# Second up projection: sixteen units instead of twelve with their weight sums formed in DRAM

## The chip, the cores and the metric

The kernel runs on one core of a Trainium2 chip. Its metric is the device time of one execution in microseconds (us); the time given for a kernel is the median of several runs. One further execution was recorded by the hardware profiler, and all rows of a trace come from that one.

## The reference, cut to what matters

A decoder layer of 512 tokens and model width 1024, in float32. The part that changes is the second feed-forward block; its hidden width is 2816, which is 22 tiles of 128.

```python
D_MODEL, SEQ, D_FF = 1024, 512, 2816

def swiglu(x, w_gate, w_up, w_down):
    return (jax.nn.silu(x @ w_gate) * (x @ w_up)) @ w_down

def reference(x, ...):
    x = x + 0.5 * swiglu(rmsnorm(x, ffn1_norm), ffn1_wg, ffn1_wu, ffn1_wd)
    x = x + hybrid_mixer(rmsnorm(x, mix_norm), w_in, ...)        # attention and a gated recurrence
    x = x + 0.5 * swiglu(rmsnorm(x, ffn2_norm), ffn2_wg, ffn2_wu, ffn2_wd)
    return rmsnorm(x, final_norm)
```

## The kernel before, in words

**Exact products from rounded parts.** TensorE multiplies float32 values that are rounded (float32r). Each operand is split into a rounded part and a remainder: ScalarE copies the rounded part (`wh`), VectorE subtracts to get the remainder (`wl`). A product is then three matmuls: `wh` with the moving rounded part, `wh` with the moving remainder, `wl` with the moving rounded part.

**Stages.** First up projection, first down projection, then the mixer as a list of 64 projections (`ORDER`, numbered 0 to 63, run by `run_jobs`), then the second up projection (`ffn_up` with `blocks`), then the second down projection. An ordinary mixer projection is 24 matmuls of 512 columns.

**The second up projection.** Of its 22 tiles, 4 (`DIRECT2`) are multiplied directly, gate and up, which makes 8 direct projections. The other 18 tiles are taken in pairs by a seven-product block scheme (as Strassen and Winograd do): two pairs of 128 columns of weights form four blocks a11, a12, a21, a22, and the tokens are halved likewise. This gives 18 *units*; each has seven *products*, numbered 1 to 7, and each product needs one block or one sum of blocks: 1 needs a11, 2 a12, 4 a22, 5 s1 = a21 + a22, 6 s2 = s1 + a11, 3 s4 = s2 + a12, and 7 s3 = a21 + a11 (the signs lie in the operands). Products 1, 6, 7 and 4 of a unit use the bank of PSUM called `mm`; 2, 5 and 3 use `aux`. The 18 x 7 = 126 products run in one list, `stream`: product i is issued, then `step(i)` reads the results of product i - 1 and calls `prepare(i + LEAD)` (`LEAD` is 4), which splits the weights of a product four places ahead.

**Two kinds of unit.** Constant `UNITS` says from which unit on the sums are formed in DRAM.

- A unit below it forms its sums in the on-chip memory. `load` has SP issue its loads (a11 and a12, a21 twice, a22: 1.25 MB), POOL adds a22 and a11 onto the two copies of a21 by accumulating DMAs, and VectorE adds s2 and s4 (`add_weights`). Only products 2, 5 and 3 are *wide*. A wide product is, for each of four operand tiles, one matmul of 512 columns (rounded part and remainder lie side by side) and one of 256; a narrow one is three matmuls of 256 columns.
- A unit from it on (`o.blocks`) reads finished sums from DRAM, 256 KB for each product, and all seven products are wide. `fetch_pair` has SP load two products' weights into one 512 KB buffer of a ring of three (`RAWS`); ScalarE and VectorE split the two together, one `wh` and one `wl` of 1024 columns; then the buffer is loaded again, for the pair three further on. Results pass through `copies` and `reads`, in place of `results`: ScalarE first copies the whole bank, VectorE then adds.

**How the DRAM sums are made.** `Blocks.stages` lists 8 DMAs of 256 KB in six dependent stages for a unit, *moves* here; for the second up projection all are issued by POOL. `sums_in_turn` interleaves the units so that two stages of one unit lie two groups apart. `sums_until(part)` issues moves until that part of them is out. It begins with a *beat*: VectorE sets one column of a small tile (8 columns in turn) and POOL copies it, so that POOL can't run ahead of VectorE. It is called at three places: in the mixer from projection `SUMS_FROM` on, twice in each projection, up to `SUMS_PART`, in proportion to the planned time since that projection over `SUMS_TIME`; six times beside the direct projections, up to `SUMS_PART + DIRECT_PART`; and at every second product of the stream, up to all of them at product `SUMS_STEPS`. The first of the six calls stands ahead of the POOL DMAs that complete the moving operands t1, r and q (`Operands.moved`, rows `cm<-ca`, `cm<-cr`, `cm<-cq`), which products 5, 7 and 4 read. The beats and moves are unknown to the planner (`Plan`), which places the mixer's other instructions by estimated times.

The sums of the second down projection's weights are moves too (`scr<-w2d` and `scr<-scr`). They are spread over the projections before `SUMS_FROM` by `run_jobs`; what is left of them is issued at projection `SUMS_FROM - 1`.

Of the kernel before, what the change touches and what calls it, by code (L numbers as in the profile page):

```python
# [44 lines left out]
PLAIN, PAIRS, TAIL = 6, 8, 3  # L45
DIRECT1, DIRECT2 = 4, 4
SUMJOBS = 48
UNITS, SUMS_FROM, SUMS_PART, DIRECT_PART, SUMS_STEPS, SUMS_TIME = 6, 37, 0.8, 0.1, 44, 145


ORDER = """
# [2022 lines left out]
```

## Time and profile before

| | us |
|---|---|
| median of 3 runs (lowest, highest) | 1062.77 (1062.4, 1063.34) |
| the profiled execution, whole | 1061.5 |
| its span, first to last instruction | 1059.7 |
| TensorE busy in the span | 1051.1 (99%) |
| VectorE busy | 884.9 (84%) |
| ScalarE busy | 667.1 (63%) |
| POOL busy | 237.2 (22%) |

Times in rows are counted from the start of the span. The span is 1.8 us shorter than the profiled execution, and that one is 1.3 us under the median. PE is TensorE's matmuls and PEld its weight loads, DVE is VectorE, ACT ScalarE; SPq is SP's queue. Matmuls overlap, so that the pitch from one start to the next tells more than the duration of one.

### The profile page before, as it was taken

What the parts mean: (1) busy time and instruction counts of PE and PEld (TensorE: products, weight loads), DVE (VectorE), ACT (ScalarE), POOL (GpSimd) and SP (SyncE); (2) the same over time, 40 slices, a digit from 0 to 9 for tenths busy, and PEclk for the clock granted to TensorE, in tenths of its full rate; (3) what the DMA queues carried; (4) which work ended last, traced back from release to release, by engine and by line L of the source; (5) the groups of instructions that cost most, each with busy time, mean ns of one, the idle gap of its engine ahead of it and who ended that gap; (6) DMA issues with size and microseconds to landing.
All of it is one profiled execution on the core that took longest, in us unless ns stands there. A gap on an engine that the chain in (4) does not pass through costs nothing.

```text
span 1059.7 us, 16590 instructions
## 1 busy us (share of the span) xinstructions
PE 1051.1 (99%) x5716; PEld 909.6 (86%) x5716; DVE 884.9 (84%) x1742; ACT 667.1 (63%) x1250; POOL 237.2 (22%) x357
## 2 busy tenths in 40 slices
PE   9999999999999999999999999999999999999997
PEld 7889999989999788888888888888899888888885
DVE  6679999989988879999899866865799888878875
ACT  7456656656476657976886664445666666666663
POOL 0261323302131011212031444442732000000020
PEclk9999999999999999999999999999999999999999
DMA  9786999938783477667494878999994666545573
GB/s 326 180 170 159 264 225 231 233 97 236 182 220 122 128 225 171 179 181 188 126 234 123 208 177 198 278 236 261 265 223 100 191 197 197 180 155 167 187 205 122
DMA packets 94548, 205.26 MB, mean 194 GB/s; under 512 B 11776, under 2 KB 18560, under 8 KB 93824
## 3 DMA queue, kind: packets, MB, share of 16 engines
q1 hardware_dynamic: 60720, 136.24, 39.2%
q0 software_dynamic: 33024, 67.13, 32.9%
q8 instruction: 45, 0.74, 0.3%
q10 hardware_dynamic: 720, 0.84, 0.2%
q14 instruction: 39, 0.32, 0.1%
HBM read 194.72 MB, written 48.23 MB: 229 GB/s over the span
## 4 chain that ended last, share of the span: by engine, by line
PE 97%; ACT 1%; DVE 1%; DMA 0%; issue 0%
PE mm L171 68%; PE aux L171 29%; DMA vt<-vec 0%; ACT L171 0%; ACT rl L171 0%; ACT r L171 0%; DVE tu L171 0%; DVE o L171 0%; DVE wl L171 0%; ACT wh L171 0%; DVE tg L171 0%; ACT yh L171 0%; DVE xr L171 0%; DVE sq L171 0%; ACT xc L171 0%
## 5 line engine op out<-in xcount | busy, mean ns | idle before, releaser
L171 DVE TENSOR_TENSOR wl<-wr,wh 128x1024 fp32r<-128x1024 f32 (+2 forms) x233 | 232.2, 1000 | 60.5 <-ACT wh L171 58.8
L171 ACT ACTIVATE wh<-wr 128x1024 fp32r<-128x1024 f32 (+3 forms) x235 | 203.7, 873 | 76.4 <-PE aux L171 24.0
L171 PE MATMUL mm<-cm,wh 128*128 128x256 f32 (+1 forms) x1184 | 240.9, 310 | 0.0
L171 PEld LDWEIGHTS mm<-cm,wh 128*128 128x128 f32 x1184 | 189.3, 191 | 7.3 <-ACT tu L171 0.2
L171 PE MATMUL mm<-cm,wl 128*128 128x256 f32 x736 | 172.5, 282 | 0.0
L171 PE MATMUL mm<-yh,wh 128*128 128x512 f32 (+1 forms) x416 | 163.8, 394 | 0.3 <-ACT i L171 0.2
L171 PE MATMUL mm<-yl,wh 128*128 128x512 f32 (+1 forms) x416 | 162.2, 390 | 0.0
L171 PE MATMUL mm<-yh,wl 128*128 128x512 f32 x408 | 159.2, 390 | 0.0
L171 PEld LDWEIGHTS mm<-cm,wl 128*128 128x128 f32 x736 | 130.0, 190 | 6.1
L171 PE MATMUL aux<-cm,wh 128*128 128x512 f32 (+1 forms) x472 | 122.9, 379 | 0.0
L171 PEld LDWEIGHTS mm<-yh,wh 128*128 128x128 f32 (+1 forms) x416 | 78.0, 187 | 17.1 <-ACT i L171 0.6
L171 PEld LDWEIGHTS mm<-yl,wh 128*128 128x128 f32 (+1 forms) x416 | 77.6, 187 | 15.6 <-DVE yl L171 0.5
L171 PEld LDWEIGHTS mm<-yh,wl 128*128 128x128 f32 x408 | 76.6, 188 | 16.4 <-DVE wl L171 0.2
L171 PEld LDWEIGHTS aux<-cm,wh 128*128 128x128 f32 x472 | 79.7, 189 | 9.4
L171 ACT ACTIVATE wh<-s 128x512 fp32r<-128x512 f32 x96 | 58.8, 625 | 43.3 <-DVE s L171 32.9
L171 DVE TENSOR_TENSOR wl<-s,wh 128x512 fp32r<-128x512 f32 x96 | 65.4, 688 | 14.5 <-ACT wh L171 13.8
L171 PEld LDWEIGHTS aux<-cm,wl 128*128 128x128 f32 x440 | 68.8, 189 | 8.7
L171 PE MATMUL aux<-cm,wl 128*128 128x256 f32 x440 | 74.0, 281 | 0.0
L326 POOL DMA_DIRECT2D scr<-w2d x32 | 29.6, 1003 | 175.5 <-DMA scr<-w2d 163.5
L159 POOL DMA_DIRECT2D s<-w1u x44 | 41.3, 1136 | 114.4 <-DVE wl L171 69.7
L159 POOL DMA_DIRECT2D cm<-h x16 | 13.8, 863 | 207.5 <-ACT cm L171 198.0
L171 PE MATMUL mm<-wh,cm 128*128 128x512 f32 x192 | 59.1, 389 | 0.0
(267 smaller groups left out, 2151.6 us busy)
## 6 DMA issues: line engine op xcount, KB each, us to landing
wr<-scr SPq DMA_DIRECT2D x80, 256.0 KB, 2.9
wr<-wm SPq DMA_DIRECT2D x39, 512.0 KB, 3.9
scr<-w2u POOLq DMA_DIRECT2D x72, 256.0 KB, 6.1
s<-w1u POOLq DMA_DIRECT2D x44, 256.0 KB, 7.6
scr<-scr POOLq DMA_DIRECT2D x40, 256.0 KB, 6.1
wr<-w1u SPq DMA_DIRECT2D x19, 512.0 KB, 6.2
wr<-w1d SPq DMA_DIRECT2D x18, 512.0 KB, 4.2
wr<-w2u SPq DMA_DIRECT2D x36, 256.0 KB, 2.9
```

Source lines behind the costliest of these rows:

```text
L159: return self.engine.dma_start(out, src, **kw)
L171: return call(*args, **kw)
L326: plain, adds = nc.gpsimd.dma_start, lambda o, i: nc.gpsimd.dma_start(o, i, accum_op=ALU.add)
```

## The change

Six constants change, and no other line:

```diff
 SUMJOBS = 48
-UNITS, SUMS_FROM, SUMS_PART, DIRECT_PART, SUMS_STEPS, SUMS_TIME = 6, 37, 0.8, 0.1, 44, 145
+UNITS, SUMS_FROM, SUMS_PART, DIRECT_PART, SUMS_STEPS, SUMS_TIME = 2, 33, 0.68, 0.07, 62, 185
```

Units 2 to 5 become units with sums in DRAM and seven wide products; units 0 and 1 stay as they are. The moves of this projection grow from 12 x 8 = 96 to 16 x 8 = 128. They begin at projection 33 instead of 37, at a lower rate for each us, and end at product 62 of the stream instead of 44. What is left of the down projection's moves is issued at projection 32 instead of 36.

## Rows read from the trace of the kernel before

**Rows 1.** Page, part 1: busy time and share of the span, instructions.

```profile
PE 1051.1 (99%) x5716; PEld 909.6 (86%) x5716; DVE 884.9 (84%) x1742; ACT 667.1 (63%) x1250; POOL 237.2 (22%) x357
```

**Rows 2.** Waits of engine PE over the span: total us, times, longest.

```profile
PE aux L171 <- DVE epst L171: 1.1, 1, 1.1
...
PE mm L171 <- ACT i L171: 0.2, 1, 0.2
```

**Rows 3.** Windows: PE, PEld, DVE, ACT, POOL busy; clock, DMA share, GB/s.

```profile
551.40:573.20 21.80, 21.80 (x102) 18.04 (x101) 21.48 (x42) 17.26 (x31) 0.85 (x3) 1.00 0.49 134
776.60:804.50 27.90, 27.90 (x206) 26.49 (x205) 27.22 (x60) 17.18 (x37) 10.32 (x16) 1.00 0.77 177
850.00:930.00 80.00, 80.00 (x459) 69.91 (x458) 69.65 (x102) 51.59 (x76) 0.00 (x0) 1.00 0.60 189
```

**Rows 4.** Timeline of PE: start, us, operation; a wide product and a narrow one.

```profile
772.33 1.09 PE L171 MATMUL aux<-cm,wh 128*128 128x512 f32 x4
...
773.74 0.40 PE L171 MATMUL mm<-cm,wh 128*128 128x256 f32 x2
...
775.18 0.40 PE L171 MATMUL mm<-cm,wh 128*128 128x256 f32 x2
```

**Rows 5.** Timeline of PE: first matmul of the stream, first after it.

```profile
762.37 0.40 PE L171 MATMUL mm<-cm,wh 128*128 128x256 f32 x2
...
940.02 0.82 PE L171 MATMUL mm<-ident,x 128*128 128x128 f32 x6
```

**Rows 6.** DMA queues and issues, 573 to 717: share of engines; count, size, us to landing.

```profile
q0 software_dynamic: 7275, 19.11, 59.2%
...
scr<-w2u POOLq DMA_DIRECT2D x59, 256.0 KB, 6.0
scr<-scr POOLq DMA_DIRECT2D x16, 256.0 KB, 5.7
...
wr<-w2u SPq DMA_DIRECT2D x5, 512.0 KB, 6.6
```

**Rows 7.** DMA queues and issues, 850 to 930.

```profile
q1 hardware_dynamic: 8281, 15.06, 59.5%
...
wr<-w2u SPq DMA_DIRECT2D x23, 256.0 KB, 2.9
```

**Rows 8.** DMA queues and issues, 663 to 679.

```profile
q0 software_dynamic: 817, 2.13, 56.1%
q1 hardware_dynamic: 751, 2.64, 46.6%
...
wr<-wout SPq DMA_DIRECT2D x6, 512.0 KB, 5.9
```

**Rows 9.** DMA issues, 762.3 to 850.

```profile
cm<-cq POOLq DMA_DIRECT2D x2, 128.0 KB, 9.7
```

**Rows 10.** Timeline of POOL: last move of the down projection's sums, last DMA of q.

```profile
556.12 0.82 POOL L326 DMA_DIRECT2D scr<-w2d  x1 [4.69 <-DMA scr<-scr]
...
763.93 0.86 POOL L159 DMA_DIRECT2D cm<-cq  x1 [1.40 <-ACT cm L171]
```

**Rows 11.** Timeline of all engines: a split that frees a buffer, then load, split, first matmul.

```profile
845.28 1.05 ACT L171 ACTIVATE wh<-wr 128x1024 fp32r<-128x1024 f32 x1
...
847.00 1.22 DVE L171 TENSOR_TENSOR wl<-wr,wh 128x1024 fp32r<-128x1024 f32 x1
...
848.25 3.25 SPq L159 DMA_DIRECT2D wr<-w2u  x3
...
853.49 1.05 ACT L171 ACTIVATE wh<-wr 128x1024 fp32r<-128x1024 f32 x1
...
854.57 1.23 DVE L171 TENSOR_TENSOR wl<-wr,wh 128x1024 fp32r<-128x1024 f32 x1 [0.17 <-PE mm L171]
...
858.62 0.63 PE L171 MATMUL mm<-cm,wh 128*128 128x512 f32 x2
```

**Rows 12.** Tile beat: engine, operation, count, duration min/median/max in ns, first and last start.

```profile
L1074 DVE MEMSET beat<- x62: 59/59/59, 573.1 to 822.4; 128x1 f32 x62
```

## The prediction, made before the changed kernel was timed

> **What bounds the kernel now.** I read the page's busy line first: TensorE's matmuls fill 1051.1 us of the span, 99%, VectorE 84%, ScalarE 63% [rows 1]. A busy PE says little by itself, so I went to the waits of PE: three waits, 1.1, 0.2 and 0.2 us, are all that the trace knows in the whole span, and the longest is at the start [rows 2]. Then the windows around the change: PE is busy in every microsecond of the stretch where the mixer would now start its moves, of the narrow units' stretch and of a stretch of wide units, at full granted clock [rows 3]. So the stream runs as fast as TensorE takes matmuls, and only the number and width of matmuls can shorten it. Last, the pitch of single products in the timeline: a wide one takes 773.74 - 772.33 = 1.41 us, a narrow one 775.18 - 773.74 = 1.44 us [rows 4]. The reader is to see there that three matmuls of 256 columns cost almost what one of 512 and one of 256 cost.
>
> I checked that against the whole stream. It has 126 products and lasts 940.02 - 762.37 = 177.65 us [rows 5]. Units 0 to 5 have four narrow products each, 24 in all. With 24 x 1.44 = 34.6, the other 102 have 143.1 us left, 1.403 each. So the wide pitch over many is 1.403, and there is no idle time left over in the stream to win.
>
> **The change, part by part.**
>
> *Narrow products become wide.* Products 1, 6, 7 and 4 of units 2 to 5: 16 products, 16 x (1.44 - 1.403) = 0.6 us less on TensorE, which is the path. It is the only term that shortens the path.
>
> *VectorE and ScalarE in those units.* On VectorE a unit loses s2 and s4 (two adds of 512 columns) and splits of 512 columns become half as many of 1024; it gains the adds of `reads`. ScalarE gains the copies of whole banks. I don't add it up, since both kinds of unit stand in the trace: the narrow ones keep VectorE busy 27.22 of 27.90 us and ScalarE 17.18, the wide ones 69.65 and 51.59 of 80 [rows 3], so VectorE goes from 98% to 87%, ScalarE from 62% to 64%. Nothing is gained, because PE didn't wait in either; nothing is lost, because the later units already run so.
>
> *More beats.* 62 now [rows 12]. Afterwards up to 62 in the mixer (31 projections, two calls), 6 and 31, so at most 37 more, 37 x 59 ns = 2.2 us of VectorE spread over some 300 us; its 13% of idle time in wide units covers it. In the four projections where beats are new, VectorE is busy 21.48 of 21.80 us [rows 3], and 8 beats need 0.5 us. PE doesn't wait for it there now; without cover it would cost that 0.5 us.
>
> *The mixer's moves.* 75 are issued between 573 and 717 [rows 6], and one more at the edge: 76 of 96. As the part is 0.8 x t / 145, the planned time t at the last call was 141.6 to 143.5 us. Four more projections are 96 matmuls; 102 took 21.8 us there [rows 3], and with the attention's own matmuls between them I put 23 us. So the new count is 128 x 0.68 x 165 / 185 = 77.6, thus 78. Two more moves over 23 us more time: the mixer's loads meet a thinner stream of moves than now, and PE doesn't wait there now. The stretch that becomes new to moves has its DMA engines at 0.49 [rows 3]. The down projection's last moves come at projection 32 in place of 36, but POOL has them out at 556.12 by itself, as their landings allow [rows 10]. The first beats of projection 33, some 23 us before 573.1 [rows 12], wait some 7 us for that; nothing else is queued behind them on POOL, and 8 columns of beats, two to a projection, are 23 us of slack for VectorE. Cost zero; gain zero.
>
> *Beside the direct projections.* The first of six calls brings the moves to 128 x 0.6917, so 89: a burst of 11, where it is now 3 (76 to 79). All six bring it to 96, 18 moves in place of 11. The burst stands on POOL ahead of the DMAs for t1, r and q. From rows 6 a move takes 0.592 x 144 / 75 = 1.14 us of all 16 engines. In return the loads of units 2 to 4 leave this stretch, and those of unit 5 the next. The operand with least room is q: its last DMA is issued at 763.93 and takes some 9.7 us, so it is there at 773.6 [rows 10, 9]; product 4 of unit 0, the twelfth of the stream, starts 6 x 1.44 + 5 x 1.403 = 15.7 us after 762.37, at 778.0. Room 4.4 us. The seven extra moves are 8.0 us of DMA time, but the loads that leave are 3 x 1.25 MB, and 256 KB of loads takes 0.595 x 80 / 57.4 = 0.83 us (15.06 MB are 57.4 such loads, [rows 7]): 12 us. Between a gain of nothing and 8.0 - 4.4 = 3.6 us lost I take zero.
>
> *In the stream.* Moves 97 to 128 come one at every second product, each 2.81 us, until product 62, some 849; now there are 9 in a shorter stretch. They take 1.14 / 2.81 = 0.41 of the DMA engines. From product 19 on, at 789, all products read from DRAM, and that alone takes 0.595 [rows 7]. Together 1.00, for 60 us. This is the one place where the change can hurt, so I worked out the room. A buffer is free when VectorE ends its split, at 847.00 + 1.22 = 848.22; SP loads it again from 848.25 on, with two issues for which I allow 0.4 us; a load takes 2.9 us [rows 7], so it is there at 851.5; ScalarE comes to it at 853.49 (2.0 us of room), VectorE ends its split at 855.80, and the product starts at 858.62 (2.8 us more) [rows 11]. One late load may be 4.8 us late. For late loads without end, the turn of the ring counts: three pairs, 3 x 2.81 = 8.42 us, must hold 0.4, the landing and the split, which took 855.80 - 853.49 = 2.3 us here and 848.22 - 845.28 = 2.9 there; so a landing of 5.1 to 5.7 us is the most it bears. How long will loads take beside moves? Alone 2.9 [rows 7]; beside moves that took 0.56, with loads at 0.47, 5.9 [rows 8] for 512 KB; in the worst crowd of this stretch now 9.7, as q's DMAs [rows 9]. For 0.41 I scale between the nearer two: 2.9 + 3.0 x 0.41 / 0.56 = 5.1. That is at the limit, not over it, and 4.8 us stand in reserve. I take zero, with bounds of zero and of what 9.7 would cost: a turn of 13.0 us, 21 pairs x (13.0 - 8.42) / 3 = 32, less 4.8, so 27 us.
>
> The sums themselves are early enough: move 128 is out at 849 and lands within 6 us [rows 6], and the last units' products come after 900.
>
> **Sum.** Against the profiled execution: 1061.5 - 0.6 = 1060.9, span 1059.1. The median stands 1.3 us over the profiled execution, so I predict 1062.77 - 0.6, rounded to 1062.2 us. About 0.2%, 2.1 us, is what a measurement of this kernel can tell from no change; the forecast is a quarter of it.
>
> **The rivals.**
>
> *The ring turns too slowly.* While moves and loads are both queued, each waits for packets of the other. A load's packet takes 0.595 x 80 x 16 / 8281 = 92 ns [rows 7], a move's 0.592 x 144 x 16 / 7275 = 187 ns [rows 6]. If they alternate one for one, a pair's 1.66 us of transfer gains up to 1.66 x 187 / 92 = 3.4 us, so that landings reach 6.3, the turn 0.4 + 6.3 + 2.9 = 9.6, and the stream loses 21 x (9.6 - 8.42) / 3 = 8.3, less 4.8 in reserve: 3.5 us, 1065.7. It decides from a lasting landing of about 5.7 us on; at 6.6, as five loads had [rows 6], it is 5.6 us, 1067.8. For it speaks the sum of 1.00; against it that six loads in 16 us at 0.56 and 0.47 did no harm, though their ring turns at leisure. Chance 0.15.
>
> The Trainium skill, page "DMA: Bandwidth & Descriptors", section "Queues, rings and completion order", says that each DMA engine takes turns between the queues that have work, a packet at a time; by that rule this rival is the normal case whenever a move is in flight, and the time would be its 1065.7. The rows agree that loads are slowed beside moves (5.9 against 2.9, though at twice the size), and leave open whether a move is always in the way.
>
> *The burst makes q late.* If the seven extra moves delay q by their full 8.0 us, product 4 of unit 0 waits 3.6 us: 1065.8. For it: they stand ahead of q on one queue. Against it: the loads of units 2 to 4 are gone. Chance 0.05.
>
> *TensorE gains more.* PE's waits in the whole span are 1.5 us [rows 2]. If all of them went, with the 0.6, it would be 1060.7, still within 2.1 us. So no mechanism of this kernel brings over 0.2%, only an error of mine in the pitch or of the measurement: 0.04.
>
> **How the numbers follow.** Forecast 0.76, the ring 0.15, the burst 0.05, more gain 0.04. Both slower rivals lie over 2.1 us: slower 0.20, same 0.76, faster 0.04. The range leaves out most of the gain's 0.04 and the costly half of the ring's 0.15: 1061.0 to 1066.2.
>
> **What would show it.** Right: the stream of the changed kernel lasts 177.0 to 177.1 us, PE's waits stay at three small ones, loads of `wr<-scr` between 789 and 849 land in about 5 us. The ring: landings of 6 us and more there, SP issuing at intervals over 2.81 us for each pair, PE waiting for `wl`. The burst: q's last DMA landing after 778, and PE waiting. A stream shorter than 176 us would show my pitch wrong; a change outside 717 to 940 would show that I missed an effect on the mixer.

## The result and the profile after

The changed kernel takes 1070.34 us (median of 6 runs, 1068.44 to 1072.75), the kernel before 1062.53 on the same chip (median of 6; the 1062.77 above was of 3 of them): ratio 1.0074, 95% interval 1.0059 to 1.0089. It is slower by about 7.8 us. I had predicted 1062.2, no difference that can be measured, and the time lies outside my range. The profiled execution took 1070.35, with a span of 1068.1 us (before: 1061.5 and 1059.7).

The page, part 1, and the shares of the chain that ended last, of the kernel after:

```profile
PE 1054.2 (99%) x5652; PEld 908.4 (85%) x5652; DVE 885.0 (83%) x1750; ACT 668.9 (63%) x1241; POOL 255.5 (24%) x406
...
PE 88%; DMA 5%; DVE 3%; ACT 2%; issue 1%; SPq 0%; POOL 0%; ACTq 0%; DVEq 0%; POOLq 0%
```

The 64 matmuls fewer are there, 5716 - 5652 [rows 1], and PE's share still reads 99%: the first line shows nothing of the loss. The second does. A chain that was almost PE alone, 97%, now goes through DMA, VectorE and ScalarE for a tenth of the span. Where that lies, the ends of the stream tell (timeline of PE, kernel after):

```profile
763.04 0.40 PE L171 MATMUL mm<-cm,wh 128*128 128x256 f32 x2
...
948.38 0.82 PE L171 MATMUL mm<-ident,x 128*128 128x128 f32 x6
```

The stream lasts 185.34 us, before 177.65 [rows 5]: 7.7 of the 8.4 us by which the span is longer. The other 0.7 lie ahead of the stream, 0.62 of them already ahead of the mixer, at 345 us, where the change does nothing; behind it both kernels need 119.7 us. So the mixer, with its four projections more of moves, lost nothing. Now PE's waits over the whole span of the kernel after:

```profile
PE mm L171 <- ACT c L171: 3.1, 4, 1.4
PE mm L171 <- ACT e L171: 2.1, 1, 2.1
PE aux L171 <- DVE epst L171: 1.1, 1, 1.1
...
PE mm L171 <- ACT wh L171: 0.2, 1, 0.2
```

The two first are new, 5.2 us in five waits [rows 2 for before]; the last is new too, but lies at 5 us, far ahead of the change. They name `c` and `e`, ScalarE's copies of full PSUM banks, and not the split operands I had watched. What ScalarE itself waited for between 760 and 946 (total us, times, longest):

```profile
ACT wh L171 <- DMA wr<-scr: 14.5, 10, 3.1
...
ACT wh L171 <- DMA wr<-w2u: 10.8, 8, 2.2
```

Eighteen times ScalarE stood at the rounding of a pair of operands whose load had not landed. In the rows below its bank copy starts only behind the roundings ahead of it, so the copy waits too, and PE finds no free bank. The longest of PE's stalls, from the timeline of all engines (start, duration, engine, operation; in brackets the idle time before it and what ended that):

```profile
832.75 3.26 SPq L159 DMA_DIRECT2D wr<-w2u  x3
...
837.17 1.06 ACT L171 ACTIVATE wh<-wr 128x1024 fp32r<-128x1024 f32 x1 [3.03 <-DMA wr<-scr]
...
841.04 1.06 ACT L171 ACTIVATE wh<-wr 128x1024 fp32r<-128x1024 f32 x1 [2.24 <-DMA wr<-w2u]
842.01 0.58 ACT L171 ACTIVATE e<-mm 128x512 f32<-128x512 f32 x1
...
842.64 1.35 PE L171 MATMUL mm<-cm,wh 128*128 128x512 f32 x3 [2.12 <-ACT e L171]
```

SP issues from 832.75 on, ScalarE waits for one pair until 837.17, for the next until 841.04, and only then copies `e`, for which PE has been idle 2.12 us. The load that ended the second wait is in the chain of waits, between the DMA's start and its landing, with a move of a sum ahead of it:

```profile
829.10 3.56 DMA scr<-w2u
832.75 0.33 SPq L159
833.12 7.82 DMA wr<-w2u
841.04 1.06 ACT wh L171
```

7.82 us, for 256 KB that took 2.9 alone [rows 7]. DMA queues and issues from 789 to 866, kernel after (share of 16 engines; count, size, median us to landing):

```profile
q1 hardware_dynamic: 7416, 13.50, 53.8%
q0 software_dynamic: 2406, 6.42, 40.0%
...
wr<-scr SPq DMA_DIRECT2D x28, 256.0 KB, 5.4
wr<-w2u SPq DMA_DIRECT2D x22, 256.0 KB, 5.5
```

The moves take the 0.40 I had reckoned, and the loads' landing has nearly doubled. Finally the windows of the kernel after (columns as in [rows 3]): beside the direct projections, the stretch with moves, the rest of the stream, and the 3.5 us behind the longest stall:

```profile
763.00:789.00 26.00, 26.00 (x179) 24.15 (x179) 22.78 (x50) 17.23 (x36) 13.83 (x23) 1.00 0.94 190
789.00:866.00 77.00, 73.19 (x402) 63.02 (x401) 61.37 (x113) 44.48 (x68) 21.20 (x48) 0.98 0.94 260
866.00:948.30 82.30, 80.90 (x462) 70.54 (x461) 70.28 (x103) 52.64 (x78) 0.00 (x0) 1.00 0.62 194
842.90:846.40 3.50, 3.50 (x12) 2.88 (x12) 3.06 (x7) 2.67 (x5) 0.99 (x2) 0.52 0.72 225
```

PE is busy through the first stretch, idle 3.8 us in the second and 1.4 in the third. In the last row the clock granted to TensorE is 0.52, its lower level of 1.2 GHz, though PE is busy all the time: 3.5 x 0.48 = 1.7 us lost that no wait shows. Without stalls the stream would last 177.65 - 0.6 = 177.05 by the prediction; a ring of four buffers (e5, below) gives 177.09. The loss is 185.34 - 177.09 = 8.25 us. Laid beside e5's stream matmul by matmul, the delay grows by 6.0 us at the five stalls, by 1.6 in the stretch of lower clock, and by 0.6 in small steps elsewhere. The five stalls show 5.2 us of idle time; the start of the matmul behind each of them is later by some 0.16 us more, since the recorded ends of matmuls are modelled.

For the ring I worked out from the single issues and landings how long a buffer's turn is, from one issue to the next into the same buffer (means over the pairs that have both issues in the stretch). The last column is the mean time from one pair's issue to the next pair's:

```
                        issue to both landed + landed to next issue = turn,  pair to pair
before, 855 to 930                 3.47      +        5.00          = 8.47,  2.82
after, 794.5 to 866                6.28      +        2.97          = 9.25,  3.02
moves slower, 800 to 890           5.25      +        3.55          = 8.80,  2.92
four buffers (e1), 794.5 to 866    6.55      +        4.33          = 10.89, 2.72
four buffers (e5), 794.5 to 866    6.25      +        5.01          = 11.26, 2.79
```

A pair of wide products needs 2 x 1.403 = 2.81 us. Of 2.8 us by which landings became longer, 2.03 came out of the time that a full buffer waits for its use, and 0.78 made the turn longer: 2.97 us between landing and next issue is about what the split itself takes (2.3 to 2.9 in [rows 11]). The 71.5 us hold 23.6 pairs, each 3.02 - 2.81 = 0.21 us too slow: 5 us. This is no further term of the loss: the stretch holds PE's stalls from 805 to 843 and the lower clock, which hold up the splits and so the ring in their turn.

### The profile page after: what moved, and what is told of

The parts are those of the page before. It is cut to its first block, busy times and chain, and to the rows that moved or that the text cites. A ratio compares the mean times of both kernels' runs of the same rounds, so it can differ in the third digit from the quotient of the medians.

```text
span 1068.1 us, 16536 instructions
## 1 busy us (share of the span) xinstructions
PE 1054.2 (99%) x5652; PEld 908.4 (85%) x5652; DVE 885.0 (83%) x1750; ACT 668.9 (63%) x1241; POOL 255.5 (24%) x406
## 4 chain that ended last, share of the span: by engine, by line
PE 88%; DMA 5%; DVE 3%; ACT 2%; issue 1%; SPq 0%; POOL 0%; ACTq 0%; DVEq 0%; POOLq 0%
PE mm L171 63%; PE aux L171 25%; DMA wr<-scr 3%; DVE wl L171 1%; ACT wh L171 1%; DMA wr<-w2u 1%; DVE tu L171 0%; DVE c L171 0%; DMA scr<-w2u 0%; DMA wr<-w1u 0%; ACT L171 0%; DVE h L171 0%; DVE tg L171 0%; ACT rl L171 0%; DVE hl L171 0%
## 5 line engine op out<-in xcount | busy, mean ns | idle before, releaser
L171 DVE TENSOR_TENSOR wl<-wr,wh 128x1024 fp32r<-128x1024 f32 (+2 forms) x244 | 247.0, 1016 | 70.0 <-ACT wh L171 68.1
L171 ACT ACTIVATE wh<-wr 128x1024 fp32r<-128x1024 f32 (+3 forms) x246 | 216.2, 884 | 100.4 <-PE aux L171 23.6
L171 PE MATMUL mm<-cm,wh 128*128 128x256 f32 (+1 forms) x1120 | 236.8, 320 | 5.2 <-ACT c L171 3.1
L171 PEld LDWEIGHTS mm<-cm,wh 128*128 128x128 f32 x1120 | 181.1, 191 | 15.3 <-ACT c L171 3.9
L171 PE MATMUL mm<-cm,wl 128*128 128x256 f32 x736 | 165.0, 282 | 0.0
L171 ACT ACTIVATE wh<-s 128x512 fp32r<-128x512 f32 x80 | 48.9, 626 | 36.5 <-DVE s L171 26.2
L171 DVE TENSOR_TENSOR wl<-s,wh 128x512 fp32r<-128x512 f32 x80 | 54.8, 690 | 14.3 <-ACT wh L171 13.7
L1075 POOL COPY beat<-beat 128x1 f32<-128x1 f32 x87 | 29.6, 340 | 154.0 <-DVE beat L1074 143.4
```

Source lines behind the costliest of these rows:

```text
L171: return call(*args, **kw)
L1075: nc.gpsimd.tensor_copy(paces[-1], paces[-1])
```

## The experiments

Medians, ratio to the kernel before with its 95% interval, and the stream in the profiled execution. Each ratio is to the kernel before as timed beside the run: 1062.09 us for e1 to e4, 1062.01 for e5 to e8, and 1063.15, one run, for e9.

| kernel | us | ratio | stream |
|---|---|---|---|
| before | 1062.53 | | 177.65 |
| after | 1070.34 | 1.0074 (1.0059 to 1.0089) | 185.34 |
| e1: four load buffers | 1064.11 | 1.0025 (1.0016 to 1.0035) | 177.26 |
| e2: before, with moves among wide products | 1068.86 | 1.0061 (1.0046 to 1.0076) | 184.31 |
| e3: all moves ahead of the stream | 1063.56 | 1.0012 (1.0003 to 1.0021) | 177.55 |
| e4: moves spread to product 90 | 1068.24 | 1.0063 (1.0046 to 1.0080) | 181.0 |
| e5: four load buffers, the fourth from the operands' slots | 1062.12 | 0.9998 (0.9989 to 1.0007) | 177.09 |
| e6: rounding of loaded pairs on GpSimd | 1147.25 | 1.0798 (1.0783 to 1.0812) | |
| e7: the new units, the old schedule | 1064.24 | 1.0021 (1.0012 to 1.0030) | 178.65 |
| e8: the old units, the new schedule | 1065.10 | 1.0028 (1.0017 to 1.0039) | 181.08 |
| e9: before, with bursts of moves | 1066.84 (one run) | | |

Four theories stand in the expectations. A: loads land late beside moves, and three buffers are too few for that landing. B: the DMA engines are full, so that no number of buffers helps. C: it isn't the moves at all; the wide units cost something by themselves. O, formed after the first runs: it is the order on ScalarE, where the bank copies stand behind the rounding, so that a single late load costs much earlier than my reserve of 4.8 us said.

### Four load buffers (e1)

```diff
-SLOTS = 60
+SLOTS = 58
+    raw4 = ctx.enter_context(tc.tile_pool(name="raw4", bufs=1))
-                r = pairs[i // 2] = raw.tile([P, WMAX], F32, tag="raw", name=nm("wr"))
+                own = i // 2 % 4 == 3
+                r = pairs[i // 2] = (raw4 if own else raw).tile([P, WMAX], F32, tag="raw4" if own else "raw", name=nm("wr"))
-                    fetch_pair(i + 2 * RAWS)
+                    fetch_pair(i + 8)
```

The last line stands at two places.

> The changed kernel with a fourth weight buffer for the pairs of the second up projection (two slots of another pool given up for it); the moves stay as they are. Theory A (the turn of the ring: a load beside moves lands after some 6 us, so three buffers can't turn in 8.42 us, ScalarE waits for the load, and its copies of the banks, which TensorE needs, queue behind): four buffers have 11.2 us for a turn of about 9, so the stream takes 177 to 178 us and the time is 1062 to 1063 us. Theory B (the sum of the demands is over what the DMA engines give): a deeper ring changes little, 1068 to 1071. Theory C (the loss comes from units 2 to 5 being wide and read from the ring, with split work and copies at the transition, not from moves): 1066 to 1071.

Measured: 1064.11, stream 177.26, and no wait of PE in it. PE's only new wait in the span lies in the mixer, where the two slots given up are missing:

```profile
PE mm L171 <- DVE atl L171: 1.2, 2, 0.9
```

The stream begins 2.3 us later than before, at 764.65, which is what remains of the loss. Moves, units and DMA bytes are those of the changed kernel, so B and C can't explain why the stalls are gone.

### Moves among the wide products of the kernel before (e2)

```diff
+    spare = [t for g in sums_in_turn(weight_blocks(w2u, DIRECT2, 14).values(), 2) for t in g]
+                if blocks and i >= 60 and i % 2 == 0 and spare:
+                    c = i // 2 % 8
+                    nc.vector.memset(beat[:, c:c + 1], 0.0)
+                    nc.gpsimd.tensor_copy(beat[:, c:c + 1], beat[:, c:c + 1])
+                    move, o_, s_ = spare.pop(0)
+                    move(o_, s_)
```

32 moves that nothing needs, at every second product from 60 on, where the kernel before has none.

> The kernel before, with 32 more moves that nothing needs (four units' sums formed once more in spare DRAM tiles), one at every second product from product 60 of the stream on. Units 2 to 5 stay narrow. Theories A and B: the loss of the changed kernel comes back without its wide units, +6 to +9 us, 1068 to 1072. Theory C: no loss, 1062 to 1063.

Measured: 1068.86, stream 184.31, 6.7 longer. Three stalls, in PE's timeline:

```profile
898.60 1.20 PE L171 MATMUL mm<-cm,wh 128*128 128x512 f32 x4 [0.56 <-ACT e L171]
...
919.68 1.19 PE L171 MATMUL mm<-cm,wh 128*128 128x512 f32 x4 [1.13 <-ACT e L171]
...
940.79 2.07 PE L171 MATMUL mm<-cm,wh 128*128 128x512 f32 x4 [2.62 <-ACT e L171]
```

The granted clock is at its lower level again from the end of the third on, from 940.4 to 943.8. Moves alone, in units that were wide already, make the loss: C falls. The beats that go with the moves are not the cause, for e1 has them too. The ring's pair takes 2.93 us here (848 to 940), with 5.47 from issue to landing.

### All moves ahead of the stream (e3), and moves spread further (e4)

```diff
-UNITS, SUMS_FROM, SUMS_PART, DIRECT_PART, SUMS_STEPS, SUMS_TIME = 2, 33, 0.68, 0.07, 62, 185
+UNITS, SUMS_FROM, SUMS_PART, DIRECT_PART, SUMS_STEPS, SUMS_TIME = 2, 33, 0.86, 0.14, 62, 165
```

> The changed kernel with all its 128 moves out before the stream: 0.86 of them in the mixer at a planned 165 us, the other 0.14 beside the direct projections. The stream is the same, without moves. Theories A and B: the stream takes 177 to 178 us; 1062 to 1063 if the mixer bears 0.67 moves for each us. Theory C: 1068 to 1071.

Measured: 1063.56, stream 177.55, pairs landing after 3.62 us. The loss goes from the stream to the mixer, which lasts 418.9 us instead of 417.35; PE's waits there are

```profile
PE mm L171 <- DVE ml L171: 0.6, 1, 0.6
PE mm L171 <- ACT mh L171: 0.4, 1, 0.4
```

So the mixer, which took 78 moves at no loss in the changed kernel, doesn't take the 110 of this one.

```diff
-UNITS, SUMS_FROM, SUMS_PART, DIRECT_PART, SUMS_STEPS, SUMS_TIME = 2, 33, 0.68, 0.07, 62, 185
+UNITS, SUMS_FROM, SUMS_PART, DIRECT_PART, SUMS_STEPS, SUMS_TIME = 2, 33, 0.68, 0.07, 90, 185
```

> The changed kernel with the stream's 32 moves spread over 90 products in place of 62, one for each 3.95 us: moves and loads together want 0.29 + 0.60 = 0.89 of the DMA engines. Theory B: under 1, so no loss, 1062 to 1063. Theory A: loads land in between, 5 to 5.5 us, and part of the loss stays, 1063 to 1067. Theory C: 1068 to 1071.

Measured: 1068.24 (1066.83 to 1070.0); the profiled execution is the fastest of them, with a stream of 181.0 and these waits of PE in it:

```profile
PE mm L171 <- ACT c L171: 1.5, 3, 0.6
PE mm L171 <- ACT e L171: 1.2, 1, 1.2
```

B falls, since the engines have room here (0.56 for loads and 0.31 for moves from 789 to 885). But A's number is missed as well: a thinner stream of moves should have cost 1 to 5 us, and it costs 6. The mean landing of a pair, 5.25, is under the 5.5 to 6.1 that the ring bears by my own sum, and PE stalls four times all the same. What a mean hides, as I read it, is that a late load costs and an early one gives nothing back: its pair waits for its turn on ScalarE. Of the 27 pairs that the mean is taken over, 11 took over 5.7 us, and the latest 7.3.

### Four buffers without taking slots from the mixer (e5)

Two tiles of 128x512 from the pool of operand slots, which has room in the stream, serve as the fourth buffer:

```diff
+                own = i // 2 % 4 == 3
+                r = None if own else raw.tile([P, WMAX], F32, tag="raw", name=nm("wr"))
+                halves[i // 2] = [slot(F32, "ws") if own else r[:, n * H:(n + 1) * H] for n in range(2)]
...
+                    if pairs[i // 2] is None:
+                        for n in range(2):
+                            wsplit(halves[i // 2][n], *(t[:, n * H:(n + 1) * H] for t in units[-1]))
...
-                    fetch_pair(i + 2 * RAWS)
+                    fetch_pair(i + 8)
```

> The changed kernel with a ring of four, but the fourth buffer is two tiles of the slot pool, whose size stays 60; each fourth pair is split in two halves. It is the run with the fourth buffer again, without the two slots taken from the mixer. Theory A (the turn of the ring): the stream takes 177 to 178 us and the mixer is as long as before, so 1061.4 to 1062.4 us, at most 0.7 us faster than the kernel before. If the mixer's loss in that run had another cause than the slots, 1063.5 to 1065.

Measured: 1062.12 against 1062.01 of the kernel before; the interval, 0.9998 ± 0.0009, contains no difference. Timeline of PE, first matmul of the stream and first behind it:

```profile
763.02 0.40 PE L171 MATMUL mm<-cm,wh 128*128 128x256 f32 x2
...
940.11 0.49 PE L171 MATMUL mm<-ident,x 128*128 128x128 f32 x3
```

177.09 us: the 0.56 that 16 narrower products cost are gone, and so is the whole loss. Now the engines under it, window and queues from 789 to 850:

```profile
789.00:850.00 61.00, 61.00 (x349) 53.29 (x348) 54.07 (x107) 40.80 (x66) 19.29 (x44) 1.00 0.99 286
```

```profile
q1 hardware_dynamic: 6499, 11.83, 56.8%
q0 software_dynamic: 2042, 5.56, 41.5%
...
wr<-scr SPq DMA_DIRECT2D x19, 256.0 KB, 5.1
wr<-w2u SPq DMA_DIRECT2D x13, 256.0 KB, 5.8
...
ws<-scr SPq DMA_DIRECT2D x6, 256.0 KB, 6.8
ws<-w2u SPq DMA_DIRECT2D x6, 256.0 KB, 5.8
```

The reader is to see that loads land as late as in the changed kernel (`ws` is the fourth buffer), that the DMA engines are fuller, 0.99 against 0.93 in the same window, and that PE is busy in all 61 us. Full engines and landings of 5 to 6 us are harmless when a pair may take four times 2.81 us to come round. This settles A against B. Whether the 0.56 us in the stream arrive in the kernel's time can't be told from these runs.

### Rounding on GpSimd (e6)

```diff
-                    wsplit(pairs.pop(i // 2), *units[-1])
+                    r = pairs.pop(i // 2)
+                    nc.gpsimd.tensor_scalar(units[-1][0], r, 1.0, None, op0=ALU.mult)
+                    V.tensor_sub(units[-1][1], r, f(units[-1][0]))
```

It was to take the loaded pairs off ScalarE, so that no bank copy stands behind them.

> The changed kernel, three buffers, the moves as they are; the rounded part wh of a pair that is formed whole is made by POOL in place of ScalarE, so that ScalarE waits for no load there and its copies of the banks don't queue behind one. Theory O (TensorE stalls early because the copies queue behind the waiting split; the turn of the ring would be forgiven for longer): the waits of PE for copies c and e go, and the loss falls from 8 to 1 to 4 us, 1063 to 1066. Theory R (the turn of the ring alone sets the loss, whoever waits): the loss stays, 1068 to 1071, with PE waiting for wl. If POOL takes well over 1.1 us for 1024 columns, the turn is longer and both give more.

Measured: 1147.25. Instructions by line on POOL, 765 to 1000 (count, busy us, mean ns):

```profile
L535 POOL TENSOR_SCALAR wh<-wr 128x1024 fp32r<-128x1024 f32 x49 | 145.9, 2997 | 6.2 <-PE aux L171 2.0 <-DVE tu L171 1.7 <-DMA wr<-scr 1.4
```

One rounding takes 3.0 us on GpSimd and 1.06 on ScalarE, longer than the 2.81 us that a pair has. PE waits for these roundings 17.7 + 16.1 us in 22 waits, and the run says nothing on O.

### The two halves of the change (e7, e8)

e7 is the kernel before with `UNITS = 2` alone, e8 the changed kernel with `UNITS = 6`.

> The kernel before with UNITS at 2 and the other five numbers as they were: 128 moves, of which 102 fall to the mixer (0.71 for each us), 13 beside the direct projections and 13 to the stream until product 44. Theory A: the loss goes with the moves beside ring loads; 13 in place of 32 give 1 to 3 us in the stream, and the mixer may lose 1 to 2 us at the higher rate: 1063 to 1066. Theory C (the wide units themselves): 1068 to 1071.

Measured: 1064.24. The stream lasts 178.65, 1.55 over e5's, with 13 moves in it, 9 of them from 789 on, and the mixer, with more moves in each us, loses 1.1. PE's waits between 570 and 960:

```profile
PE mm L171 <- ACT c L171: 1.0, 2, 0.7
PE mm L171 <- DVE ml L171: 0.6, 1, 0.6
```

> The kernel before with the five new numbers of the schedule and UNITS still 6: 96 moves, 24 of them in the stream until product 62. The ring is read from product 40 on, so about 8 moves stand beside ring loads. Theory A: 0 to +2 us, 1062 to 1064. If moves in the stream cost something whatever they stand beside: +4 to +6 us.

Measured: 1065.10, more than I expected. Here the narrow units stay, and PE waits for them, at 783 and 786:

```profile
PE mm L171 <- DVE wl L171: 2.1, 2, 1.4
```

DMA issues of that kernel from 762 to 800:

```profile
q0 software_dynamic: 2865, 4.86, 69.3%
...
s<-w2u POOLq DMA_DIRECT2D x6, 256.0 KB, 10.4
a<-w2u SPq DMA_DIRECT2D x5, 256.0 KB, 11.0
...
s<-w2u SPq DMA_DIRECT2D x4, 256.0 KB, 11.1
```

In the same stretch of the kernel before those three took 6.7, 9.6 and 9.2 us. The new schedule's moves are also in the way of narrow units; the changed kernel shows no such wait, and its units 2 to 5 are no longer narrow. The two halves cost 2.2 and 3.1 us, together 7.8, more than their sum: only together do 24 moves stand beside ring loads from 789 on, where e7 has 9 and e8, whose ring starts at some 815, has 11.

### How late may one load be (e9)

Four bursts of spare moves in the kernel before, each at one product, far apart:

```diff
+    stages = [u.stages(nc.gpsimd) for u in weight_blocks(w2u, DIRECT2, 14).values()]
+    spare = [m for s in range(2) for u in stages for m in u[s]]
+                burst = {58: 2, 72: 3, 86: 4, 100: 6}.get(i, 0) if blocks else 0
+                if burst:
...
+                    for _ in range(burst):
+                        move, o_, s_ = spare.pop(0)
+                        move(o_, s_)
```

> The kernel before with four bursts of spare moves that nothing needs (2, 3, 4 and 6 of them, issued at once at products 58, 72, 86 and 100 of the stream, where there are no other moves). Each makes a few loads late, once, so that the room of one load is read directly. The prediction's reckoning (a load has 2.0 us before ScalarE and 2.8 more before the product, 4.8 in all): the bursts of 2 and 3 cost nothing; TensorE stalls only where a load takes over 2.9 + 4.8 = 7.7 us. Theory O (ScalarE waits in order, and its copies of banks, which the next but one product needs, stand behind the split): TensorE stalls from a landing of about 6 us on, and waits for copies c or e, not for wl. In all 1 to 6 us, 1063 to 1068.

Measured: 1066.84 in one run, 1063.15 for the kernel before beside it. The latest load of the first three bursts landed after 4.2, 3.8 and 6.1 us. In the last burst the loads of three pairs in a row were late: 7.4 and 9.07, 9.2 and 10.8, 9.5 and 9.9 us. Nothing stalled in the first three bursts; ScalarE's longest waits in the third and the last, then PE's:

```profile
897.53 1.06 ACT L171 ACTIVATE wh<-wr 128x1024 fp32r<-128x1024 f32 x1 [1.17 <-DMA wr<-scr]
...
919.95 1.06 ACT L171 ACTIVATE wh<-wr 128x1024 fp32r<-128x1024 f32 x1 [3.94 <-DMA wr<-scr]
...
923.90 1.06 ACT L171 ACTIVATE wh<-wr 128x1024 fp32r<-128x1024 f32 x1 [1.89 <-DMA wr<-scr]
```

```profile
922.06 1.18 PE L171 MATMUL mm<-cm,wh 128*128 128x512 f32 x4 [1.04 <-ACT c L171]
...
925.50 1.92 PE L171 MATMUL mm<-cm,wh 128*128 128x512 f32 x4 [1.79 <-ACT c L171]
```

A load of 6.1 us, 3.2 later than alone, makes ScalarE wait 1.17 us and PE not; the difference, 2.0, is the room ahead of ScalarE that the prediction had. One of 9.07, the first pair's, stalls PE by 1.04 us, so the reserve of one late load is 9.07 - 2.9 - 1.04 = 5.1 us, against the 4.8 I had worked out. O's early threshold falls, on this one load of 6.1; what is right in O is the way in which lateness reaches PE, through the bank copy `c`. The second stall, 1.79 us, comes 3.4 us later, from the next pair, whose load took 10.8: the reserve was spent and had not come back.

## Why the prediction was wrong

*What bounds the kernel, and the gain.* Right. The stream was as fast as TensorE takes matmuls, and 16 narrow products made wide are worth about the 0.6 us predicted: 0.56 in e5's stream of 177.09, though 0.39 in e1's and 0.10 in e3's, one trace each.

*VectorE, ScalarE, beats, the mixer's moves.* Right, zero each. The mixer's length is unchanged within 0.1 us. That this was near an edge I didn't see: in e3 and e7 a denser row of moves costs the mixer 1.6 and 1.1 us.

*Beside the direct projections.* Right, zero: q's last DMA lands by 772.3, and PE is busy from 763 to 789. The rival in which the burst makes q late didn't come about.

*In the stream.* This step failed, in three things. First the size: I scaled a load's landing to 5.1 us, 5.5 with the issue, between a row of 256 KB loads and one of 512 KB, and a pair took 6.28. Second, a mean at the limit was counted as free. e4's mean of 5.25 is under the limit and its stream still loses 3.9 us; by e5 it is the depth of the ring, not the engines' share of 1.00, that has to cover the scatter. Third, the 4.8 us in reserve. It is a true figure for one late load (5.1 in e9), read where the ring had long been turning, and I took it off the whole loss. It was not there when the crowd began. PE's first stall stands behind the pair that SP issued at 786.43; ScalarE had split the pair before it at 785.78, and no other loaded pair was in hand. Rows of the kernel after (chain, then timelines of ScalarE and PE):

```profile
786.81 5.51 DMA wr<-scr
...
792.42 1.06 ACT L171 ACTIVATE wh<-wr 128x1024 fp32r<-128x1024 f32 x1 [3.08 <-DMA wr<-scr]
...
794.01 1.19 PE L171 MATMUL mm<-cm,wh 128*128 128x512 f32 x4 [1.07 <-ACT c L171]
```

The pair took 5.88 us with the issue, less than the mean, and cost 1.07 us all the same. From there on the reserve never came back: a full buffer's time until its next issue was 2.97 us in place of 5.00, and each late load came on top of the last.

*The rival that came about* is "the ring turns too slowly", with 0.15, at the place that I named and from the landing that I named. It gave 1065.7, and 1070.34 was measured, so its price was too low as well. Its turn of 9.6 us (measured 9.25) made 8.3 us, from which I took the reserve of 4.8; what was lost is 8.25, of which 5.2 is idle time of PE and 1.7 the lower clock behind the longest stall, a term I didn't have. That 8.3 without the reserve is so near to 8.25 is luck: the measured turn gives 21 x (9.25 - 8.42) / 3 = 5.8, and the clock is no part of it. The sign I looked for, PE waiting for `wl`, was the wrong one: it waits for the bank copies.

The prediction quoted the Trainium skill, page "DMA: Bandwidth & Descriptors", section "Queues, rings and completion order": a DMA engine takes turns between the queues that have work, a packet at a time. The trace agrees better with the estimate made by alternating packets one for one, 6.3 us for a pair and 6.7 with the issue, than with my scaling, 5.5: it has 6.28 with the issue, and single loads of 5.4 in the median and 7.8 at worst. No run shows the turns themselves, but I should have given this rival far more than 0.15.

What stays open: why runs of the changed kernel spread over 4.3 us and those of the kernel before over 1.2 (the pattern of late loads may differ from run to run; I have one trace of it); how the loss depends on the rate of moves, since e4, with moves at 0.31 of the DMA engines in place of 0.40, still lost 6.2 us of 7.8; and what the order on ScalarE costs by itself, since e6 did not test it.

## What to carry to other kernels

Size a ring of buffers by the landing under load and its scatter, not by the mean: in this kernel three buffers, 3 x 2.81 = 8.42 us, were too few for landings of 6.28 and a use of 2.97, and four, 11.24 us, were enough. Don't take the room that one late load has off a lasting loss: here it was spent, or not yet there, when the crowd began. When a transfer queue becomes crowded, try one more buffer before less traffic; here a fourth one made 0.99 busy DMA engines harmless, and moves at three quarters of the share took off a fifth of the loss. Look at what stands behind the instruction that waits for a load on its engine: here that was the bank copy, and it is what PE missed.

## What the runs showed of the hardware

A short stall can cost more than itself. Behind PE's stall of 2.12 us in the changed kernel the granted clock was at 1.2 GHz for 3.4 us, and as long behind 2.62 us in e2 and 1.79 us in e9 (3.4 us after one of 1.04). Behind the stall of 1.40 us in the changed kernel and that of 1.13 in e2 it stayed at 2.4 GHz.

256 KB loads landed after 2.9 us alone, and after 4.2, 3.8, 6.1 and 10.8 us at worst beside 2, 3, 4 and 6 moves of 256 KB issued at once. From 789 to 850 us, four buffers moved 286 GB/s with the DMA engines at 0.99 (e5), where three moved 259 at 0.93 (after).

GpSimd's rounding of 128x1024 elements took 2997 ns, ScalarE's 1060.
